# Projection stage of a hybrid encoder layer: gates in turns with two units, heads queued behind products, the gMLP gate's input kept in SBUF, five late units behind the norm

## The chip, the cores and the metric

The kernel runs on one core of a Trainium2 chip. The metric is the device time of one execution in microseconds; less is better. Three runs of the kernel before took 1433.87, 1438.87 and 1436.48 us, median 1436.48. One execution was also profiled.

The engines are named as the profile names them: PE is TensorE (matmuls), PEld its weight load, DVE VectorE, ACT ScalarE, POOL GpSimd, SP SyncE, which issues all transfers here. Every engine runs its own instructions in order, and so does SP with its queue of transfers.

## The reference

One layer of a streaming encoder for two request groups, 1024 prompt tokens and 32 sample tokens, with the same weights, all in float32:

```python
mod = silu(c) @ w_ada + b_ada
sh1, sc1, g1, sh2, sc2, g2 = split(mod, 6)
h = x * (1 + sc1) + sh1
mq, mk, mv, mo, mi, mf, fq, fk, fv, ff, gu, gv = split(h @ w_in)
hm = head_norm(mlstm(mq, mk / 8, mv, mi, log_sigmoid(mf))) * norm_g * sigmoid(mo)   # 4 heads of 64, a carried state
hf = softmax(fq fk^T / 8 + F_t - F_s, causal) fv                                    # 8 heads of 64, F = cumsum(log_sigmoid(ff))
vn = layer_norm(gv);  hg = gu * (tril(ws) @ vn + bs)                                # gMLP, in blocks of 128 tokens
x = layer_norm(ALPHA * x + (1 + g1) * (concat(hm, hf, hg) @ w_o))
h = x * (1 + sc2) + sh2
x = layer_norm(ALPHA * x + (1 + g2) * ((silu(h @ w_gate) * (h @ w_up)) @ w_down))
```

The width is 1024, the inner width of the last line 2816. Outputs are x, the new keys, values and log-forget values, the mlstm state, and vn of the sample tokens.

## The kernel before

The program is recorded with a scheduler: the code below gives a priority by the place at which an instruction is written, and the scheduler makes of it one fixed order for each engine. What stands in the code first therefore need not run first; what counts is the order on each engine.

**Products.** Every float32 operand is split into a high and a low part, so a product is three matmuls for each of the 8 slices of 128 rows (k): high by high, high by low, low by high (`gemm`, lines 114 to 116; in `tm_unit` lines 279 to 281). Weights come 512 KB at a time into one of three `raw` buffers; ACT casts the high part (line 102, `whi`) and DVE or POOL subtracts the low part (line 103, `wlo`), three buffers each.

**The stages, in the order of time.** (1) `fm_first` streams x, makes h and multiplies the first unit. (2) The projection stage: units of 128 or 256 weight columns (`fm_unit` with the features on partitions, `tm_unit` with the tokens on partitions), the gates (`gates`, lines 383 to 491, chains of small DVE operations), the pieces of the modulation (`ada`), and, with high priority between them, the attention heads for the first 512 tokens (`fox`, f0 to f7) and the mlstm blocks m0 to m3. The string `ORDER` gives their written order: q0 to q7 are the units of queries and keys of a head, k0 and k1 the mlstm keys, s the state's loads, v and o the mlstm values and output gates, a one piece of the modulation. Then follow four units of the gMLP part, two for its gate input gv (`evac_gv`) and two for gu (`evac_gmlp`), over nine tiles of tokens. (3) `wo(0)`: the output projection for the first 512 tokens, in 8 steps m, two cuts of 256 tokens. (4) The first norm (`ln1`), with "late units" as fill for PE. A late unit is the second token group's part (512 to 1056) of the queries and keys of one head; only the heads below `QD` = 2 do both groups at once. Of the six late units `PRE` - `QD` stand ahead of `wo`, the rest behind the norm. (5) The FFN (`up`, `down`) with the other attention chunks between its products, then the same for the second group.

**Around wo.** Heads, mlstm and gMLP store their results to DRAM (`dmix0` for the first 512 tokens, `dmix1` for the others), the mlstm blocks and the gMLP through two transposes and a copy (`to_mix`, lines 623 to 634, tiles `mlstm_t` and `mixs`). `wo_res` loads the residual x into z (tile `mlstm_z`, eight loads of 256 KB), `wo_mix` loads the 16 tiles of 128 x 256 through four buffers (`wo_tmp`) and splits them into `mlstm_ah` and `mlstm_al` (lines 884 and 885). `wo` uses k in the order

```python
KORDER = (2, 3, 4, 5, 0, 1, 6, 7)
```

where 2 to 5 are the attention heads, 0 and 1 mlstm, 6 and 7 gMLP. After each step, `sublayer_end` adds the result to z (line 923), before it the pivot of the norm is subtracted on POOL (line 920).

**The gate input.** `evac_gv` normalises a tile on DVE, scales and shifts it on POOL (lines 350, 351) and stores it to `dvn` in DRAM; `evac_gmlp` loads it again (tile `gvn`) for its four small matmuls (line 646).

Of the kernel before, what the change touches and what calls it, by code (L numbers as in the profile page):

```python
# [33 lines left out]
PRE = 4  # L34
# [8 lines left out]
ORDER = "q0 f0 q1 a f1 a q2 f2 k0 k1p s a q3 f3 a v q4 f4 a q5 f5 o a m0 q6 f6 a m1 q7 m2 f7 a m3"  # L43
# [24 lines left out]
class Kernel:  # L68
# [39 lines left out]
    def gemm(self, ps, w, cols, xh, xl, start=True, stop=True):  # L108

        nc = self.nc  # L110
        n = len(w)
        for k in range(n):
            hi, lo = w[k][0][:, cols], w[k][1][:, cols]
            nc.tensor.matmul(ps, hi, xh(k), start=start and k == 0, stop=False)  # L114
            nc.tensor.matmul(ps, hi, xl(k), start=False, stop=False)  # L115
            nc.tensor.matmul(ps, lo, xh(k), start=False, stop=stop and k == n - 1)  # L116
# [223 lines left out]
    def evac_gv(self, tt, ps, n):  # L340
# [7 lines left out]
        v = self.t(self.sm, [P, 256], F32, "traw", 2)  # L348
# [3 lines left out]
        self.store(self.dvn[:n, tt, :], v[:n])  # L352
# [30 lines left out]
    def gates(self):  # L383
# [19 lines left out]
        nc.vector.scalar_tensor_tensor(p, p, 1.0, s, ALU.add, ALU.mult)  # L403
        nc.vector.tensor_scalar(a, z, 0.0, None, ALU.min)
# [3 lines left out]
        self.store(d["o_lfs"], ls[:NS, 8, 4:12])  # L408
        gs = t([P, 9, 96], "gs")
# [8 lines left out]
        for j0 in (0, 4, 8):  # L418
# [6 lines left out]
            nc.scalar.copy(rb[:, j0:j0 + nj, :].rearrange("p j q -> p (j q)"), ps[:96, :nj * P])  # L425

# [4 lines left out]
        for j in range(8):  # L431
# [7 lines left out]
            self.store(self.dfs[:, :, j * P:(j + 1) * P], f(fr[64:72]))  # L439
        nc.vector.tensor_copy(self.sf[64:72, :], rb[64:72, 8, 0:NS])  # L440

# [6 lines left out]
        for i in range(7):  # L448
            w = 1 << i
            dst = tmp[i % 2]  # L450
            nc.vector.tensor_tensor(dst[:, :, w:], src[:, :, w:], src[:, :, :P - w], ALU.max)
            nc.gpsimd.tensor_copy(dst[:, :, :w], src[:, :, :w])
            src = dst
        A = src
# [16 lines left out]
        self.store(d["o_ms"], mes)  # L471
        m0x = t([4, 9], "m0x")
# [39 lines left out]
    def mlstm(self, j):  # L512
# [97 lines left out]
        sq = t([P, 4, 64], "msq")  # L610
# [304 lines left out]
    def sublayer_end(self, c, z, m, ps, gate, st, a, b):  # L915
# [3 lines left out]
        if pivot and m:  # L919
            self.nc.gpsimd.tensor_tensor(z[:, m, sl], z[:, m, sl], st["pv"][:, sl], ALU.subtract)  # L920
# [6 lines left out]
        if st and st["sum"]:  # L927
# [125 lines left out]
    def run(self):  # L1053
# [9 lines left out]
        self.dvn = t([P, 9, 256], "dvn")  # L1063
# [52 lines left out]
        self.gates()  # L1116
        more(T1[3])
        s2 = ExitStack()
# [3 lines left out]
        def emit(x):  # L1122
# [7 lines left out]
            if x[0] == "q":  # L1130
                self.fm_unit(w3[2 + i], self.evac_qk(i), (0, 1) if i < QD else (0,), eng)
            elif x[0] == "k":
                self.fm_unit(w3[i], self.evac_mqk(2 + i, 0.125), eng=eng)
# [36 lines left out]
        for h in range(QD, PRE):  # L1170
            self.fm_unit(w3[2 + h], self.evac_qk(h), (1,))
# [10 lines left out]
        for h in range(PRE, 8):  # L1182
            self.fm_unit(w3[2 + h], self.evac_qk(h), (1,))
# [179 lines left out]
```

## Time and profile before

| | us |
|---|---|
| median of 3 runs | 1436.48 |
| lowest and highest run | 1433.87, 1438.87 |
| the profiled execution | 1436.1 |
| its span, first to last instruction | 1434.3 |
| PE busy in it | 1385.6 (97%) |
| DVE busy | 960.7 (67%) |
| ACT busy | 641.3 (45%) |
| POOL busy | 254.3 (18%) |
| mean granted TensorE clock | 0.986 |

How to read the views. A group's row has the line of the code, the engine, the operation, the tiles it writes and reads, their shapes, the count, and then busy us, mean ns and the idle time ahead of it. "PE fm_g L114 <- DVE fm_qkl L364" in the waits means that PE's matmul at line 114 waited for DVE's instruction at line 364. Matmuls are pipelined: one of 256 columns takes about 0.28 us from start to end, but the next starts 0.12 us after it. The clock is the share of the full TensorE clock that was granted, 1.00 at the best.

### The profile page before, as it was taken

The page shows a single profiled execution, that of the slowest core. Times are in us where ns is not written, and L with a number is a line of the kernel's source. Part 1 is how long each engine was busy: PE and PEld are TensorE (multiplying, and loading weights), DVE is VectorE, ACT ScalarE, POOL GpSimd, SP SyncE. Part 2 cuts the span into 40 slices and gives each one's busy share as a digit, 9 for nine tenths or more (in the row PEclk, how much of TensorE's full clock was granted, in tenths as well). Part 3 has the DMA queues.
Part 4 walks back from the last instruction along what each step waited for, and adds up shares of the span by engine and source line. Part 5 has one row for each costly group of instructions (what it writes and reads, how often), then busy time and mean ns, then how long its engine had stood idle before and what let it go on. Part 6 is the DMA issues. An engine that isn't in the chain of part 4 may idle for free.

```text
span 1434.3 us, 28877 instructions
## 1 busy us (share of the span) xinstructions
PE 1385.6 (97%) x11141; PEld 1336.3 (93%) x11141; DVE 960.7 (67%) x2220; ACT 641.3 (45%) x1405; POOL 254.3 (18%) x295
## 2 busy tenths in 40 slices
PE   7999999999999899999999999999999999999994
PEld 4899988989899889999999998999999999999994
DVE  5558655678688777687767765668857545454676
ACT  3323244434445564546555353436745342424353
POOL 0103100043157300000000002254500000000433
PEclk9999999999999999999999999999999999999997
DMA  9754678565654755443443533522224222222431
GB/s 359 253 210 128 200 206 259 160 197 168 224 176 151 215 161 178 115 145 120 126 139 104 101 104 67 196 89 74 100 73 153 89 89 89 89 89 89 133 104 63
DMA packets 120867, 207.35 MB, mean 145 GB/s; under 512 B 21380, under 2 KB 76300, under 8 KB 120728
## 3 DMA queue, kind: packets, MB, share of 16 engines
q1 hardware_dynamic: 120728, 205.49, 45.9%
q8 instruction: 88, 1.44, 0.4%
q14 instruction: 51, 0.42, 0.1%
HBM read 173.78 MB, written 31.66 MB: 143 GB/s over the span
## 4 chain that ended last, share of the span: by engine, by line
PE 82%; DMA 7%; DVE 6%; ACT 1%; issue 1%; SPq 1%; POOL 1%; DVEq 0%; ACTq 0%; POOLq 0%
PE up_g L115 8%; PE up_g L116 8%; PE up_g L114 8%; PE dn_g L114 4%; PE dn_g L115 4%; PE dn_g L116 4%; PE up_u L116 3%; PE up_u L115 3%; PE up_u L114 3%; PE tm_g L279 2%; PE tm_g L280 2%; PE tm_g L281 2%; PE fox_t L729 2%; PE wo_g L114 2%; PE wo_g L115 2%; PE wo_g L116 2%
## 5 line engine op out<-in xcount | busy, mean ns | idle before, releaser
L114 PE MATMUL up_g<-wo_ah,up_whi 128*128 128x256 f32 (+1 forms) x1008 | 288.8, 287 | 3.4 <-ACT lna_tmp L942 3.3
L115 PE MATMUL up_g<-wo_al,up_whi 128*128 128x256 f32 (+1 forms) x1008 | 290.4, 288 | 0.4 <-DVE wo_al L945 0.4
L116 PE MATMUL up_g<-wo_ah,up_wlo 128*128 128x256 f32 (+1 forms) x1008 | 289.4, 287 | 0.0
L114 PEld LDWEIGHTS up_g<-wo_ah,up_whi 128*128 128x128 f32 x1008 | 191.4, 190 | 4.9 <-ACT wo_ah L944 3.5
L115 PEld LDWEIGHTS up_g<-wo_al,up_whi 128*128 128x128 f32 x1008 | 191.6, 190 | 1.3 <-DVE wo_al L945 0.7
L116 PEld LDWEIGHTS up_g<-wo_ah,up_wlo 128*128 128x128 f32 x1008 | 191.3, 190 | 0.4 <-DVE up_wlo L103 0.2
L102 ACT CAST up_whi<-up_raw 128x1024 fp32r<-128x1024 f32 x94 | 98.5, 1047 | 143.1 <-PE dn_u L115 53.8
L103 DVE TENSOR_TENSOR up_wlo<-up_raw,up_whi 128x1024 fp32r<-128x1024 f32 x94 | 121.1, 1288 | 61.0 <-ACT up_whi L102 60.7
L114 PE MATMUL dn_g<-up_acth,dn_whi 128*128 128x256 f32 (+1 forms) x464 | 133.8, 289 | 2.4 <-DVE mlstm_z L923 2.4
L115 PE MATMUL dn_g<-up_actl,dn_whi 128*128 128x256 f32 (+1 forms) x464 | 132.3, 286 | 0.0
L116 PE MATMUL dn_g<-up_acth,dn_wlo 128*128 128x256 f32 (+1 forms) x464 | 132.1, 285 | 0.0
L116 PE MATMUL up_u<-wo_ah,up_wlo 128*128 128x272 f32 (+1 forms) x400 | 115.4, 289 | 0.0
L114 PE MATMUL up_u<-wo_ah,up_whi 128*128 128x272 f32 (+1 forms) x400 | 114.9, 287 | 0.0
L115 PE MATMUL up_u<-wo_al,up_whi 128*128 128x272 f32 (+1 forms) x400 | 114.5, 286 | 0.0
L280 PE MATMUL tm_g<-tm_wlo,start_h1h 128*128 128x256 f32 (+1 forms) x384 | 111.3, 291 | 0.0
L281 PE MATMUL tm_g<-tm_whi,start_h1l 128*128 128x256 f32 (+1 forms) x384 | 111.0, 290 | 0.0
L279 PE MATMUL tm_g<-tm_whi,start_h1h 128*128 128x256 f32 (+1 forms) x384 | 110.3, 289 | 0.2 <-ACT tm_mixs L630 0.2
L114 PE MATMUL fm_g<-start_h1h,fm_whi 128*128 128x256 f32 (+2 forms) x344 | 102.7, 304 | 5.5 <-ACT fm_whi L102 1.9
L115 PE MATMUL fm_g<-start_h1l,fm_whi 128*128 128x256 f32 (+2 forms) x344 | 102.5, 298 | 0.1
L116 PE MATMUL fm_g<-start_h1h,fm_wlo 128*128 128x256 f32 (+2 forms) x344 | 101.4, 296 | 0.0
L114 PEld LDWEIGHTS dn_g<-up_acth,dn_whi 128*128 128x128 f32 x464 | 87.7, 189 | 3.3 <-DVE mlstm_z L923 3.0
L115 PEld LDWEIGHTS dn_g<-up_actl,dn_whi 128*128 128x128 f32 x464 | 87.8, 189 | 0.4
(447 smaller groups left out, 3806.2 us busy)
## 6 DMA issues: line engine op xcount, KB each, us to landing
up_raw<-w_gu SPq DMA_DIRECT2D x94, 512.0 KB
dn_raw<-w_dn SPq DMA_DIRECT2D x30, 512.0 KB
ada_late<-w_ada SPq DMA_DIRECT2D x24, 512.0 KB
wo_raw<-w_o SPq DMA_DIRECT2D x24, 512.0 KB
ada_araw<-w_ada SPq DMA_DIRECT2D x16, 512.0 KB
fm_raw<-w_in_f SPq DMA_DIRECT2D x16, 512.0 KB
tm_raw<-w_in SPq DMA_DIRECT2D x12, 512.0 KB
dn_raw<-w_dn SPq DMA_DIRECT2D x16, 384.0 KB
```

The source lines that it names most:

```text
L102: nc.scalar.copy(hi[:, :w], raw[:, :w])
L103: (eng or nc.vector).tensor_tensor(lo[:, :w], raw[:, :w], f(hi[:, :w]), ALU.subtract)
L114: nc.tensor.matmul(ps, hi, xh(k), start=start and k == 0, stop=False)
L115: nc.tensor.matmul(ps, hi, xl(k), start=False, stop=False)
L116: nc.tensor.matmul(ps, lo, xh(k), start=False, stop=stop and k == n - 1)
L279: nc.tensor.matmul(ps[:, :ncol], xh, hi, start=k == 0, stop=False)
L280: nc.tensor.matmul(ps[:, :ncol], xh, lo, start=False, stop=False)
L281: nc.tensor.matmul(ps[:, :ncol], xl, hi, start=False, stop=k == 7)
L729: nc.tensor.transpose(ps[:, y * P:(y + 1) * P], probs[y][:, b * P:(b + 1) * P], self.ident)
```

## The change

- **Gates in turns.** `gates` becomes a generator with fourteen stops, and `fm_unit` one with a stop after each range; the two units q0 and q1 are written in turns with the gates.
- **Heads queued behind products.** `ORDER` is new: q0 and q1 are out of it, heads stand at other places, and m3 is the last again, now without a piece of the modulation ahead of it. Each head is written with `issue_after(self.lastmm.ins)`: the scheduler may place its instructions only behind the last matmul of the last `gemm` written so far.
- **The gate input in SBUF.** The normalised tile stays in a pool of its own (`vk`, five buffers); the tensor `dvn` with its nine stores and nine loads is gone. To make room the mlstm's squares (`msq`) share the buffer of `mkw`, the weighted keys that the state's matmul reads.
- **Five late units behind the norm.** `PRE` is 3 where it was 4: one late unit stands ahead of `wo`, five behind the norm.
- **The pivot.** Where the norm's sums are not taken (the last group but one of `down`), the pivot is subtracted behind the addition instead of ahead of it.

```diff
-PRE = 4
+PRE = 3
...
-ORDER = "q0 f0 q1 a f1 a q2 f2 k0 k1p s a q3 f3 a v q4 f4 a q5 f5 o a m0 q6 f6 a m1 q7 m2 f7 a m3"
+ORDER = "f0 a q2 f1 a k0 k1p s f2 a q3 v f3 a q4 o f4 a q5 m0 f5 q6 a m1 q7 f6 a m2 f7 m3"
...
-            nc.tensor.matmul(ps, lo, xh(k), start=False, stop=stop and k == n - 1)
+            self.lastmm = nc.tensor.matmul(ps, lo, xh(k), start=False, stop=stop and k == n - 1)
...
             evac(o, n, ps[:, :n])
+            yield
+            self.phase = "fm"
...
-        v = self.t(self.sm, [P, 256], F32, "traw", 2)
+        v = self.vn[tt] = self.t(self.vk, [P, 256], F32, "vn", 5)
         nc.vector.tensor_scalar(v[:n], ps[:n, :256], mv[:n, 0:1], r[:n], ALU.subtract, ALU.mult)
         nc.gpsimd.tensor_tensor(v[:n], v[:n], self.rowp[:n, 272:528], ALU.mult)
         nc.gpsimd.tensor_tensor(v[:n], v[:n], self.rowp[:n, 528:784], ALU.add)
-        self.store(self.dvn[:n, tt, :], v[:n])
...
             nc.vector.tensor_tensor(x[:, tt, :], self.G[:, tt, :], self.rowp[:, 0:16], ALU.add)
+        yield
+        self.phase = "gates"
...
-        sq = t([P, 4, 64], "msq")
+        sq = t([P, 4, 64], "mkw")
...
-        vn = self.t(self.sm, [P, 256], F32, "gvn", 2)
-        self.load(vn[:n], self.dvn[:n, tt, :])
+        vn = self.vn[tt]
...
-        if pivot and m:
-            self.nc.gpsimd.tensor_tensor(z[:, m, sl], z[:, m, sl], st["pv"][:, sl], ALU.subtract)
+        sums = st and st["sum"]
+        less = lambda: self.nc.gpsimd.tensor_tensor(z[:, m, sl], z[:, m, sl], st["pv"][:, sl], ALU.subtract)
+        if pivot and m and sums:
+            less()
...
         if pivot and m == 0:
             self.ln_pivot(st, z, sl)
-        if st and st["sum"]:
+        elif pivot and not sums:
+            less()
+        if sums:
             self.ln_sum(st, z, m, sl)
...
-        self.gates()
+
+        def units(*hs):
+            for h in hs:
+                yield from self.fm_unit(w3[2 + h], self.evac_qk(h))
+
+        weave(self.gates(), units(0, 1))
         more(T1[3])
+        s7 = ExitStack()
+        self.vk = self.pool("vk", ctx=s7, side="right")
+        self.vn = {}
...
-            if x[0] in "fm" and HPA:
-                with tc.high_priority(HPA):
-                    weave(*[iter(emit(y)) for y in x.split("+")])
-            else:
-                weave(*[iter(emit(y)) for y in x.split("+")])
+            with ExitStack() as how:
+                if x[0] in "fm":
+                    how.enter_context(tc.high_priority(HPA))
+                if x[0] == "f":
+                    how.enter_context(tc.issue_after(self.lastmm.ins))
+                weave(iter(emit(x)))
```

What the scheduler makes of it, at two places. The first is PE around the last mlstm block, m3, and the start of the output projection. `mlstm_t` from `mlstm_mhm` are the two transposes with which m3 hands over its result; `wo_g` are the output projection's products, `fm_g` those of a late unit, `tm_g` those of the gMLP units. Before, at PE's rows 2353 to 2359, while the first wo_g stands at row 2500:

```order
L580 MATMUL mlstm_s_4280<-mlstm_mv_817_4243,mlstm_mkw_4267 128x130 x2
L628 MATMUL mlstm_t_4311<-start_ident_101,mlstm_mhm_4291 128x128 x2
L182 MATMUL ada_t_4216<-start_ident_101,ada_adas_4229 128x128 x2
L628 MATMUL tm_g_4971<-start_ident_101,tm_traw_4998 128x128 x2
L628 MATMUL tm_g_5013<-start_ident_101,tm_traw_5040 128x128 x2
L279 MATMUL tm_g_5097<-tm_whi_4961,start_h1h_151 128x256
L280 MATMUL tm_g_5097<-tm_wlo_4962,start_h1h_151 128x256
```

And in the change, at rows 2448 to 2459 (line 649 is the old line 628):

```order
L649 MATMUL mlstm_t_4292<-start_ident_100,mlstm_mhm_4272 128x128 x2
L115 MATMUL fm_g_5192<-start_h1l_151,fm_whi_5154 128x272
L116 MATMUL fm_g_5192<-start_h1h_150,fm_wlo_5155 128x272
L114 MATMUL fm_g_5192<-start_h1h_150,fm_whi_5154 128x272
L115 MATMUL fm_g_5192<-start_h1l_151,fm_whi_5154 128x272
L116 MATMUL fm_g_5192<-start_h1h_150,fm_wlo_5155 128x272
L114 MATMUL fm_g_5192<-start_h1h_150,fm_whi_5154 128x272
L115 MATMUL fm_g_5192<-start_h1l_151,fm_whi_5154 128x272
L116 MATMUL fm_g_5192<-start_h1h_150,fm_wlo_5155 128x272
L182 MATMUL ada_g_5131<-start_ident_100,ada_adas_5144 128x128 x2
L114 MATMUL wo_g_5265<-mlstm_ah_832_4318,wo_whi_5261 128x256
L114 MATMUL wo_g_5302<-mlstm_ah_832_4318,wo_whi_5298 128x256
```

m3's transposes, which had 136 product matmuls between them and the first wo_g, have 8; and the products of the steps m = 0, 1 and 2 now alternate over k (5265, 5302 and a third are their banks).

The second place is SP's queue at the same point. `start_dmix` from `mlstm_mixs` is the store of m3's result (12_68 and 11_67 are dmix0, 13_69 is dmix1), `mlstm_z` from `xT` the residual, `wo_tmp` the tiles for the output projection. Before:

```order
L88 DMA start_dmix_12_68<-fox_fr_4212 64x512
L85 DMA tm_gvn_5122<-start_dvn_63 128x256
L88 DMA start_dmix_12_68<-mlstm_mixs_4314 128x2x128
L88 DMA start_dmix_13_69<-tm_mixs_5010 128x2x128
L88 DMA start_dmix_13_69<-tm_mixs_5052 128x2x128
L85 DMA mlstm_z_837_4328<-xT 128x512 x8
L85 DMA wo_tmp_4341<-start_dmix_12_68 128x256
L85 DMA wo_tmp_4345<-start_dmix_12_68 128x256
L85 DMA wo_tmp_4349<-start_dmix_12_68 128x256
L85 DMA wo_tmp_4353<-start_dmix_12_68 128x256
L85 DMA tm_gvn_5160<-start_dvn_63 32x256
```

And in the change:

```order
L88 DMA o_kT<-fm_qkr_5185 64x272
L88 DMA start_dmix_11_67<-mlstm_mixs_4295 128x2x128
L85 DMA mlstm_z_831_4309<-xT 128x512 x8
L85 DMA wo_tmp_4322<-start_dmix_11_67 128x256
L85 DMA wo_tmp_4326<-start_dmix_11_67 128x256
L85 DMA wo_tmp_4330<-start_dmix_11_67 128x256
L85 DMA wo_tmp_4334<-start_dmix_11_67 128x256
L88 DMA start_dqh_57<-fm_qkh_5217 128x272
L88 DMA start_dql_58<-fm_qkl_5218 128x272
L88 DMA o_kT<-fm_qkr_5219 64x272
L85 DMA wo_raw_5444<-w_o 128x1024
```

In both, the residual and the tiles follow m3's store; the loads of `tm_gvn` are gone, a late unit's three stores and one weight load of the output projection stand behind the first four tiles, and the other twelve tiles follow in one piece.

More of the change, by code (lines that the diff above doesn't have):

```diff
@@ L403, in gates @@
         nc.vector.scalar_tensor_tensor(p, p, 1.0, s, ALU.add, ALU.mult)
+        yield
+        self.phase = "gates"
         nc.vector.tensor_scalar(a, z, 0.0, None, ALU.min)
@@ L408, in gates @@
         self.store(d["o_lfs"], ls[:NS, 8, 4:12])
+        yield
+        self.phase = "gates"
         gs = t([P, 9, 96], "gs")
@@ L425, in gates @@
             nc.scalar.copy(rb[:, j0:j0 + nj, :].rearrange("p j q -> p (j q)"), ps[:96, :nj * P])
+        yield
+        self.phase = "gates"
         fc = t([72, 8], "fc")
@@ L439, in gates @@
             self.store(self.dfs[:, :, j * P:(j + 1) * P], f(fr[64:72]))
+            if j % 2:
+                yield
+                self.phase = "gates"
         nc.vector.tensor_copy(self.sf[64:72, :], rb[64:72, 8, 0:NS])
+        yield
+        self.phase = "gates"
         m0s = t([4, 1], "m0s")
@@ L453, in gates @@
             src = dst
+            if i % 2:
+                yield
+                self.phase = "gates"
+        yield
+        self.phase = "gates"
         A = src
@@ L471, in gates @@
         self.store(d["o_ms"], mes)
+        yield
+        self.phase = "gates"
         m0x = t([4, 9], "m0x")
@@ L1170, in run @@
         for h in range(QD, PRE):
-            self.fm_unit(w3[2 + h], self.evac_qk(h), (1,))
+            weave(self.fm_unit(w3[2 + h], self.evac_qk(h), (1,)))
+        s7.close()
         s6.close()
@@ L1182, in run @@
         for h in range(PRE, 8):
-            self.fm_unit(w3[2 + h], self.evac_qk(h), (1,))
+            weave(self.fm_unit(w3[2 + h], self.evac_qk(h), (1,)))
         self.ln1_res(0)
```

5 lines of the change are left out of this document (2 added, 3 removed).

## The prediction

> **What bounds the kernel now.** I read the page first, then the waits of TensorE (PE), then the clock around each wait, and last the transfers ahead of the output projection.
>
> ```profile
> span 1434.3 us, 28877 instructions
> PE 1385.6 (97%) x11141; PEld 1336.3 (93%) x11141; DVE 960.7 (67%) x2220; ACT 641.3 (45%) x1405; POOL 254.3 (18%) x295
> PE 82%; DMA 7%; DVE 6%; ACT 1%; issue 1%; SPq 1%; POOL 1%; DVEq 0%; ACTq 0%; POOLq 0%
> ```
>
> PE is busy for 97% of the span and the chain that ended last runs over it. The change leaves the number of products as it is, so it can win only what PE loses in gaps, and lose only by new gaps. These are the waits of PE from 40 to 560 us, in us in total, times, longest, and below the "..." those from 860 to 900 us:
>
> ```profile
> PE up_g L114 <- ACT lna_tmp L942: 3.3, 1, 3.3
> PE fox_t L729 <- DVE fox_p L715: 2.3, 1, 2.3
> PE fm_g L114 <- DVE fm_qkl L364: 1.9, 1, 1.9
> PE fox_s L698 <- DMA fox_qp<-start_dql: 1.8, 2, 1.6
> PE tm_g L646 <- DMA tm_gvn<-start_dvn: 1.5, 1, 1.5
> PE fm_g L114 <- ACT tm_mixs L630: 0.9, 1, 0.9
> PE fox_s L698 <- DMA fox_qp<-start_dqh: 0.6, 1, 0.6
> ...
> PE dn_g L114 <- DVE mlstm_z L923: 2.4, 2, 1.8
> ```
>
> A gap costs more than itself. In the view by stretches (start:end, length, busy time and count on PE, PEld, DVE, ACT and POOL, granted clock, DMA share, GB/s) the first two rows are the gap at 139 us and what follows it; 305:309 and 473:477 hold the gaps at 306 and 474 us, and the rest follow the gaps at 242, 306, 378, 474 and 887 us:
>
> ```profile
> 138.00:142.00 4.00, 2.11 (x18) 1.91 (x17) 3.91 (x7) 0.14 (x1) 1.55 (x2) 1.00 0.30 91
> 142.00:146.00 4.00, 4.00 (x23) 4.00 (x22) 3.88 (x5) 1.87 (x4) 3.55 (x7) 0.57 0.32 93
> 245.00:249.00 4.00, 4.00 (x24) 4.00 (x24) 2.52 (x11) 1.39 (x5) 0.00 (x0) 0.62 0.94 300
> 305.00:309.00 4.00, 1.74 (x12) 1.31 (x11) 3.96 (x10) 1.28 (x4) 2.59 (x2) 1.00 0.74 226
> 309.00:313.00 4.00, 4.00 (x24) 4.00 (x22) 3.27 (x8) 0.97 (x2) 2.02 (x4) 0.57 0.77 276
> 381.00:385.00 4.00, 4.00 (x21) 4.00 (x21) 1.45 (x5) 1.13 (x3) 0.00 (x0) 0.57 0.81 263
> 473.00:477.00 4.00, 1.04 (x9) 0.83 (x8) 4.00 (x9) 2.80 (x8) 2.44 (x2) 0.96 0.10 37
> 477.00:484.00 7.00, 6.27 (x36) 5.60 (x40) 5.29 (x14) 5.47 (x15) 7.00 (x12) 0.53 0.50 144
> 890.00:894.00 4.00, 3.35 (x29) 3.15 (x28) 0.97 (x2) 0.00 (x0) 4.00 (x6) 1.00 0.66 37
> ```
>
> PE looks fully busy in 142:146, but it does 23 matmuls there at a clock of 0.57: (1 - 0.57) x 4 = 1.7 us are lost on top of the 1.9. After 242 us it is 0.38 x 4 = 1.5, after 306 and 378 us 1.7 each, after 474 us 0.47 x 7 = 3.3; after 887 us nothing (1.00). What the change can win at most is therefore 242: 1.6 + 1.5, 306: 2.3 + 1.7, 378: 1.5 + 1.7 with 0.9 just before it, 474: 3.3 + 3.3, 887: 2.4, and 0.6 at the first head: 20.8 us.
>
> **The gates in turns.** The order of all five engines is the same before and after up to PE's row 1102 (about 175 us), so the weaving of the gates with q0 and q1 moves nothing, and the gap at 139 us stays with its 1.9 + 1.7. I cost this part at 0; no other work has to hide it.
>
> **The gate input in SBUF.** Nine stores and nine loads of up to 128 KB go from SP's queue. The gap of 1.5 us is PE waiting for such a load. What the stores did to SP between 330 and 410 us:
>
> ```profile
> SPq L88 <- POOL tm_traw L351: 12.9, 5, 3.6
> ```
>
> SP, an engine in order, stood 12.9 us behind POOL's affine step, with loads queued behind the stores. Now PE waits for POOL alone, whose result is ready before any of these stores could start. I take the whole 0.9 + 1.5 + 1.7 = -4.1 (bounds -4.1 and 0). The squares of mlstm now share a buffer with mkw and wait for the state's matmul; between that one and the transposes of m3 PE has 40 late-unit products in the new order, about 5 us, that hide this. Without that cover it would be part of the new waits below.
>
> **Heads behind products.** The heads' matmuls stand later behind the products of the unit ahead. Gaps of 0.6 + 3.1 + 4.0 = 7.7 us at the heads can go; I take -5 (bounds -7.7 and 0), since a head that starts later is also packed closer to the next one. The stage's end is denser: f7 and m3 run with few products between their steps. New waits there cost what the old ones did, 3.1 to 4.0 us each with the clock. I take +2.5, less than one; bounds 0 and 8 (two).
>
> **The wait ahead of the output projection.** This is the largest term. m3 is now last, and SP issues the residual (mlstm_z) and every wo_tmp load only after m3's store. The old times of that chain, in the timeline (start, length, engine, operation; SP, ACT and PE rows, left-out rows between them):
>
> ```profile
> 365.70 0.38 PE L628 MATMUL mlstm_t<-start_ident,mlstm_mhm 128*128 128x128 f32 x2
> ...
> 366.52 0.37 SPq L88 DMA_DIRECT2D start_dmix<-mlstm_mixs  x1
> 366.98 0.96 SPq L88 DMA_DIRECT2D start_dmix<-tm_mixs  x2
> 368.03 3.76 SPq L85 DMA_DIRECT2D mlstm_z<-xT  x8
> 371.84 2.55 SPq L85 DMA_DIRECT2D wo_tmp<-start_dmix  x4
> ...
> 377.35 1.51 ACT L884 CAST mlstm_ah<-wo_tmp 128x256 fp32r<-128x256 f32 x4 [2.31 <-DMA wo_tmp<-start_dmix]
> ...
> 378.24 1.75 SPq L85 DMA_DIRECT2D wo_tmp<-start_dmix  x4
> ...
> 382.90 1.13 ACT L884 CAST mlstm_ah<-wo_tmp 128x256 fp32r<-128x256 f32 x3 [3.39 <-DMA wo_tmp<-start_dmix]
> 383.79 1.27 SPq L85 DMA_DIRECT2D wo_tmp<-start_dmix  x3
> ...
> 386.41 0.40 ACT L884 CAST mlstm_ah<-wo_tmp 128x256 fp32r<-128x256 f32 x1
> ```
>
> And wo's own matmuls in the first nine microseconds, in the view by stretches (PE, PEld, DVE, clock, DMA share, GB/s):
>
> ```profile
> 391.40:400.40 9.00, 8.67 (x72) 8.51 (x72) 0.48 (x1) 1.00 0.60 189
> ```
>
> Before, the transposes of m3 (365.70) lay 26 us ahead of wo's first matmul (391.4 to 391.5), and product work covered the chain. Now 8 products stand between. Let T be the start of m3's transposes. The store is issued at T + 0.8 (366.52 - 365.70) and takes 0.4, so the residual's first load goes at T + 1.3; the two stores of tm_mixs that stood between are gone. From there to the first cast took 377.35 - 368.03 = 9.3: T + 10.6, and with a cast and a subtraction of 0.4 each the first tile is usable at T + 11.4. There are four tmp buffers, so 16 tiles come in rounds of four. A round is 386.41 - 383.79 = 2.6 plus 0.8, or 3.4; with two 512 KB weights ahead, 382.90 - 378.24 = 4.7 plus 0.8, or 5.5. wo's products take k in the order 2, 3, 4, 5, 0, 1, 6, 7, and k = 6 and 7 are tiles 13 and 14, three rounds after the first: one weight stands in the queue, so half the extra, 11.4 + 3 x 3.4 + 1 = T + 22.6.
>
> PE is done with the 8 products at about T + 1.4 and has m = 0, 1, 2 to do: 72 products in 8.7 us by the last row, 54 of them (6.5 us) for the first six k. Unhindered it would ask for k = 6 at T + 7.9. The loss is 22.6 - 7.9 = 14.7, in two gaps of some 9 and 5 us, and the half clock of 1.7 after the second; the one after the first lies within the wait for the second. So +16.4. Low bound: tmp lands 2.6 after its issue as z's last load goes (371.84 - 368.03 + 2.6, plus 1.3: T + 7.7, usable 8.5) and rounds stay 3.4, giving 10.8. High: two rounds of 5.5 and 3.3 for the clock, giving 18 + 3.3 = 21. Queued behind on SP are only wo's later weights, which cannot be converted before m = 0 has freed its buffers.
>
> **The fifth late unit.** It leaves the stretch ahead of wo and comes back behind the norm, 5.8 us each way, so the move itself is 0. It fills the 474 us gap:
>
> ```profile
> 457.00:463.00 6.00, 6.00 (x50) 6.00 (x49) 0.50 (x1) 1.14 (x3) 1.00 0.36 113
> L364 DVE SCALAR_TENSOR_TENSOR fm_qkl<-fm_g,start_qsc,fm_qkh 128x272 fp32r<-128x272 f32 x8 | 3.9, 493 | 3.4 <-POOL mlstm_z L954 2.2 <-POOL fm_qkr L365 1.1
> L103 DVE TENSOR_TENSOR fm_wlo<-fm_raw,fm_whi 128x1024 fp32r<-128x1024 f32 x3 | 3.6, 1215 | 0.1
> ```
>
> Fifty such matmuls took 6.0 us, so a unit's 48 (two ranges, eight k, three each) take 5.8, more than the gap. But DVE is the one that is late there (4.00 of 4.00 in 473:477), and the unit gives it 1.2 + 2 x 0.5 = 2.2 us more. Of 6.6 us I take -4.6 (bounds -6.6 and -2.6).
>
> **The subtraction behind the addition.** In the down stage DVE's addition (L923) no longer waits for POOL's subtraction of the pivot where no sums follow. The 2.4 us at 887 go: -2.4 (bounds -2.4 and 0). POOL's subtraction is late next, and nobody asks for it before the last group.
>
> **The sum.** -4.1 - 5 + 2.5 + 16.4 - 4.6 - 2.4 = +2.8 on the profiled execution's 1436.1 (span 1434.3), which lies 0.4 under the runs' median of 1436.48. The forecast is 1439, a change of 0.2%: within the 0.3% (4.3 us) below which a measurement of this kernel cannot tell it from none.
>
> **The clock by the skill.** The Trainium skill, "TensorE: Matmul & The Clock Gate", Part 1, puts the halved clock behind an idle window of about 3.4 us and states the rule that PE be kept free of gaps longer than that. The trace disagrees: gaps of 1.5 to 2.3 us are followed by 0.57 to 0.62 for some 4 us. By the rule the gaps that go would be worth only themselves, and the sum would be the fourth rival's.
>
> **Rivals.** (1) *Slower: the stage's end starves.* One mechanism: f7, m2 and m3 packed in the last products ahead of wo; DVE's small steps queue, m3 comes late, and each us of that adds in full to the wait for wo because nothing covers it any more. For it speaks that DVE was at 3.96 of 4.00 where head and units met at 306 us (the row is the wait of fox_t on fox_p); against it, that DVE had idle time beside another head (2.52 of 4.00 in 245:249). It decides once m3 is over 5 us late. New waits at 8 and the wait for wo at its high 21: +2.8 + 5.5 + 4.6 = 1449. (2) *Faster: the wait is short.* The loads meet an empty queue, wo's wait costs 10.8 and all the gaps go: 10.8 - 4.1 - 7.7 + 0 - 6.6 - 2.4 = -10: 1426; with part of it, 1428. For: 300 GB/s moved at 245 us, 189 around wo; against: DVE's load behind the norm. (3) *The parts do not do what they say*: so it is for the gates, which is in every case. Were the heads' part as empty, their -5 would be gone: 1444, inside the forecast's own range. (4) *Gaps without aftermath.* If the half clock would be there without the gaps, because it comes at its own times, the wins lose 1.7 at 378, 5/7.7 of 3.2 at the heads and 4.6/6.6 of 3.3 behind the norm, 6.1 in all: 1445. Against: each of five such stretches follows a gap.
>
> **How the numbers follow.** Forecast 0.37 (its own range 1432 to 1444: same 0.22, slower 0.12, faster 0.03); rival 1 0.27, slower; rival 2 0.26, faster; rival 4 0.10, slower. Together faster 0.29, same 0.22, slower 0.49. The middle of the largest case stays the prediction. The range takes in most of rivals 1 and 2: 1427 to 1452, with a tenth left out on either side.
>
> **What would show it.** Right: PE waits in wo's first products for a wo_tmp cast, one of about 9 and one of about 5 us, some 20 us after the transposes of m3, with a clock near half behind them; the gap at 139 us unchanged; no wait on tm_gvn or on L923 near 887 us; the wait on lna_tmp under 2 us. Wrong: m3's store long ahead of wo's first matmul; or waits of PE in the heads over 8 us in sum; or a half clock without a gap before it.

## The result, and the profile after

Four runs of the changed kernel took 1444.84 to 1454.52 us, median 1450.47; four of the kernel before, median 1435.17. The ratio is 1.0098, 95% interval 1.0073 to 1.0122: the change makes the kernel slower by 1%. The time lies in the range of the prediction, at the time of its first rival, not of its forecast.

| | before | after |
|---|---|---|
| median, us | 1435.17 | 1450.47 |
| profiled execution, us | 1436.1 | 1448.55 |
| its span, us | 1434.3 | 1446.4 |
| its mean granted clock | 0.986 | 0.983 |

The head of the page, after:

```profile
span 1446.4 us, 28825 instructions
PE 1384.2 (96%) x11141; PEld 1336.1 (92%) x11141; DVE 961.5 (66%) x2220; ACT 642.4 (44%) x1405; POOL 258.2 (18%) x295
```

PE did the same 11141 matmuls and was busy for 1.4 us less, so all of the 12.1 us by which the span grew is waiting. The waits of PE from 40 to 600 us (total, times, longest):

```profile
PE wo_g L114 <- ACT mlstm_ah L904: 9.4, 2, 7.8
PE up_g L114 <- DVE fm_qkl L365: 3.5, 1, 3.5
PE fox_s L718 <- DMA fox_k<-start_dqh: 3.0, 1, 3.0
PE fox_o L754 <- DVE fox_ptl L753: 2.0, 1, 2.0
PE fox_s L719 <- DMA fox_k<-start_dql: 2.0, 1, 2.0
PE fm_g L114 <- DVE fm_qkl L365: 2.0, 1, 2.0
PE ada_g L182 <- ACT ada_adas L179: 1.7, 1, 1.7
PE fox_s L719 <- DMA fox_k<-start_dqh: 1.4, 1, 1.4
```

The first row is new and the largest: the output projection waits for its tiles. The second stands where the old wait on lna_tmp stood and is as long; the third, the first mixer head's wait for its keys, is new. The waits on tm_gvn and, near 887 us, on the addition into z are gone. The sixth is the gap at 139 us, unchanged. Here is the chain ahead of the output projection, from the timeline (PE, ACT and SP rows; line 649 is the old 628, line 904 the old 884):

```profile
381.12 0.38 PE L649 MATMUL mlstm_t<-start_ident,mlstm_mhm 128*128 128x128 f32 x2
...
381.93 0.38 SPq L88 DMA_DIRECT2D start_dmix<-mlstm_mixs  x1
382.36 3.98 SPq L85 DMA_DIRECT2D mlstm_z<-xT  x8
...
386.38 2.15 SPq L85 DMA_DIRECT2D wo_tmp<-start_dmix  x4
...
391.94 1.45 ACT L904 CAST mlstm_ah<-wo_tmp 128x256 fp32r<-128x256 f32 x4 [7.83 <-DMA wo_tmp<-start_dmix]
...
402.81 1.88 ACT L904 CAST mlstm_ah<-wo_tmp 128x256 fp32r<-128x256 f32 x4 [1.12 <-DMA wo_tmp<-start_dmix]
...
403.27 0.62 PE L114 MATMUL wo_g<-mlstm_ah,wo_whi 128*128 128x256 f32 x3 [1.60 <-ACT mlstm_ah L904]
```

With T = 381.12 the residual's loads start at T + 1.2 (forecast 1.3), the first cast at T + 10.8 (10.6), and PE gets k = 6 at T + 22.2 (22.6). The stretches there and behind the norm, with the clock in the third column from the end:

```profile
384.00:393.00 9.00, 1.04 (x5) 0.81 (x6) 3.32 (x13) 1.17 (x5) 0.97 (x2) 0.54 0.98 331
393.00:397.00 4.00, 4.00 (x20) 4.00 (x20) 0.87 (x3) 0.56 (x3) 0.00 (x0) 0.50 0.77 252
404.00:408.00 4.00, 3.13 (x22) 2.58 (x22) 3.23 (x6) 3.45 (x5) 0.00 (x0) 1.00 0.00 0
142.00:146.00 4.00, 4.00 (x23) 4.00 (x23) 3.88 (x5) 2.00 (x4) 3.48 (x6) 0.57 0.32 93
```

While PE stood, the DMA engines were at 0.98 of their time and moved 331 GB/s: the wait is transfers. The first products then ran at half clock (0.50), which cost nothing of its own, because the next tiles were not there before 403 us.

Where the 12.1 us came from, at equal work. Wo's last matmul starts at 441.4 us before and 446.5 after, the first matmul of down at 540.7 and 553.0; k = 6 before is reckoned as 391.5 + 6.5. A late unit's 48 matmuls, 5.8 us, moved from ahead of the output projection to behind it, so 5.8 is added to times ahead of it and taken from the stretch behind:

| stretch of the profiled execution | before | after | difference at equal work |
|---|---|---|---|
| start to the end of the products ahead of wo | 391.5 | 382.5 | 382.5 + 5.8 - 391.5 = -3.2 |
| from there to wo's k = 6 | 6.5 | 20.8 | +14.3 |
| from k = 6 to wo's last matmul | 43.4 | 43.2 | -0.2 |
| to the first matmul of down | 99.3 | 106.5 | 7.2 - 5.8 = +1.4 |
| to the end | 893.6 | 893.4 | -0.2 |

These are two executions, one of each kernel. The point-by-point part below sets them beside executions of other runs, and there the first row does not hold.

### The profile page after: what moved, and what is told of

Read it like the earlier page. It is cut to its first block, busy times and chain, and to the rows that moved or that the text cites. A ratio compares the mean times of both kernels' runs of the same rounds, so it can differ in the third digit from the quotient of the medians.

```text
span 1446.4 us, 28825 instructions
## 1 busy us (share of the span) xinstructions
PE 1384.2 (96%) x11141; PEld 1336.1 (92%) x11141; DVE 961.5 (66%) x2220; ACT 642.4 (44%) x1405; POOL 258.2 (18%) x295
## 4 chain that ended last, share of the span: by engine, by line
PE 84%; DMA 6%; DVE 5%; ACT 2%; SPq 1%; issue 1%; POOL 1%; DVEq 0%; ACTq 0%; POOLq 0%
PE up_g L116 8%; PE up_g L115 8%; PE up_g L114 8%; PE dn_g L114 4%; PE dn_g L115 4%; PE dn_g L116 4%; PE up_u L116 3%; PE up_u L115 3%; PE up_u L114 3%; PE tm_g L281 3%; PE tm_g L282 3%; PE tm_g L283 3%; PE fm_g L114 3%; PE fm_g L115 2%; PE fm_g L116 2%; PE fox_t L749 2%
```

## The experiments

Twelve kernels were run, in three groups of four beside runs of the kernel before (medians 1437.1 to 1437.6 us there). The change itself was not run again beside them. Differences to it are between medians of different groups; by the ratios they come out the same within 0.5 us. The waits and stage times of a run are those of its one profiled execution, which lay up to 6.3 us from the run's median (u_pre: 1435.49 us, x_res2: 1439.18, both the fastest of their run).

| run | median us | ratio to before, 95% interval |
|---|---|---|
| x_res | 1449.69 | 1.0091 (1.0073 to 1.0109) |
| u_order | 1441.34 | 1.0037 (1.0019 to 1.0056) |
| u_pre | 1441.78 | 1.0037 (1.0016 to 1.0058) |
| vn_pivot | 1436.63 | 1.0002 (0.9989 to 1.0015) |
| x_res2 | 1444.59 | 1.0057 (1.0032 to 1.0083) |
| vn_pivot_res2 | 1436.81 | 1.0003 (0.9988 to 1.0018) |
| o_pre | 1439.99 | 1.0017 (1.0000 to 1.0033) |
| o_pivot | 1434.34 | 0.9973 (0.9958 to 0.9988) |
| u_pre_res2 | 1446.51 | 1.0067 (1.0048 to 1.0086) |
| o_order | 1445.01 | 1.0058 (1.0037 to 1.0080) |
| o_vn | 1444.96 | 1.0054 (1.0036 to 1.0071) |
| pivot_norm | 1435.76 | 0.9986 (0.9965 to 1.0007) |

**x_res: the residual's loads behind the first tile loads, in the changed kernel.**

```diff
-        self.wo_res(0, self.pz)
         self.operand(0, self.ph)
         self.wo_mix(0, self.KORDER[:6])
+        self.wo_res(0, self.pz)
```

> The changed kernel with one thing other: the sixteen tile loads for the output projection (wo_tmp) are written ahead of the eight residual loads (mlstm_z), so that SP issues the tiles right behind m3's store. Theory 1, the wait ahead of the output projection is the transfer chain behind m3's store: without the 2.1 MB ahead of them the first tiles land about 6 us earlier (3.8 us of issue and the moving), so the first wait of 7.8 us falls to about 2 us and the kernel takes about 1444 us. Theory 2, m3 itself is late and the transfers matter little: the wait stays over 6 us and the time at 1449 to 1452. Theory 3, most of the loss sits in the heads and behind the norm: the wait falls, but the time by less than 3 us.

1449.7 us, no gain. The waits of PE in this run:

```profile
PE wo_g L114 <- ACT mlstm_ah L904: 7.4, 2, 6.7
```

There are still two waits, but the long one is now the second. m3's transposes came 3.3 us later in this execution (T = 384.4 us); the output projection starts at T + 4.2 instead of T + 11.3 and its last matmul at T + 64.0 instead of T + 65.4. SP's rows show why: the scheduler put two of the eight residual loads behind the first four tiles, three behind eight and three behind twelve, so that the whole 2.1 MB still stood ahead of the last four tiles. By its numbers theory 2 held (7.4 us of wait, 1449.7 us), but the edit took the residual only out of the first tiles' way and put it in the later ones': it moved the wait and tells nothing of its cause. x_res2 below moves it further back.

**u_order: the old ORDER in the changed kernel.**

```diff
-ORDER = "f0 a q2 f1 a k0 k1p s f2 a q3 v f3 a q4 o f4 a q5 m0 f5 q6 a m1 q7 f6 a m2 f7 m3"
+ORDER = "f0 a f1 a q2 f2 k0 k1p s a q3 f3 a v q4 f4 a q5 f5 o a m0 q6 f6 a m1 q7 m2 f7 a m3"
```

> The changed kernel with the old ORDER (heads and mlstm blocks at their old places, q0 and q1 with the gates as in the change). m3's transposes then have 48 product matmuls behind them ahead of the output projection instead of 8, 40 x 0.12 = 4.8 us more cover. Theory 1 (the wait is what costs): the wait of 7.8 us falls to about 3 us, and the new waits in the heads (1.4, 2.0, 0.8 and 2.0 us, with their half clock) go back to the old ones: 1440 to 1445. Rival (the order is not the cause; the five late units and the norm are): 1448 to 1452.

1441.3 us, 9 us less than the change, in the range of theory 1. The wait for the tiles is 8.4 us in sum, not 3, but it falls earlier: wo's last matmul is at 437.6 instead of 446.5 us, because the heads' waits are smaller (PE's waits from 40 to 375 us are 6.1 us in sum; in the change 10.9, in x_res and x_res2 with the same order 8.7 and 10.5) and the products ahead of wo are done at 375.5 us instead of 382.5 (x_res 385.8, x_res2 380.9). From there to wo's last matmul it takes 62.1 us, in the change 64.0: the gain lies ahead of wo, not at the tiles. So the time came as expected and half of the reason given for it did not.

**u_pre: PRE = 4 in the changed kernel.**

```diff
-PRE = 3
+PRE = 4
```

> The changed kernel with PRE = 4: two late units ahead of the output projection, four behind the norm, as before. 48 matmuls (5.8 us) more stand between m3's transposes and the output projection. Theory 1: the first wait falls from 7.8 to about 2 us, and the unit's 5.8 us are taken back behind the norm, where the old gap of 3.3 us with its half clock returns: -6 for the wait, 0 to +3 behind the norm, 1444 to 1447. Rival (the fifth unit behind the norm costs by itself, by the wait of up_g on fm_qkl of 3.5 us and the first mixer head's wait of 3.0 us for its keys): 1440 to 1443.

1441.8 us, 8.7 less than the change: less time than theory 1 had, in the range of its rival. What both name is in the trace. wo's last matmul comes at 443.0 us against 446.5 + 5.8 = 452.3 at equal work, so the unit ahead covers transfers; and the wait of up_g on fm_qkl is gone and that of the first mixer head down to 0.7 us, while the old one on lna_tmp (3.4 us) is back. The profiled execution is 6.3 us faster than the run's median, so these stages tell where the gain lies and not how large it is.

**vn_pivot: the kernel before with the gate input in SBUF and the pivot behind the addition.**

```diff
+        v = self.vn[tt] = self.t(self.vk, [P, 256], F32, "vn", 5)
-        self.store(self.dvn[:n, tt, :], v[:n])
-        sq = t([P, 4, 64], "msq")
+        sq = t([P, 4, 64], "mkw")
+        vn = self.vn[tt]
...
+        elif pivot and not sums:
+            less()
```

> The kernel before with two parts of the change alone: the gate input in SBUF (with the shared buffer of the squares) and the subtraction of the pivot behind the addition. If the parts are worth what the prediction took them for, -4.1 and -2.4: about 1429 us, the gaps at 374, 378 and 887 us gone, and m3's transposes still 96 matmuls (11.5 us) ahead of the output projection, which nearly covers its loads. Rival: the gate input's tiles move other work, a new wait of the same size comes in its place and only the pivot's 2.4 us stay: about 1433 us. Third: m3 later than before opens a wait ahead of the output projection of some 5 us: about 1435 to 1438 us.

1436.6 us, as before. The waits on tm_gvn and at 887 us are gone, and PE waits 5.0 us for the first tile of the output projection: m3's transposes stand 96 instead of 136 matmuls ahead of it. That is the third expectation, in wait and time.

**x_res2: the residual's loads written behind all tile loads, in the changed kernel.**

```diff
-        self.wo_res(0, self.pz)
         self.operand(0, self.ph)
...
         self.wo_mix(0, self.KORDER[6:])
+        self.wo_res(0, self.pz)
```

> The changed kernel with the residual's loads (mlstm_z) written behind all sixteen tile loads of the output projection; the run before had them behind the first four or so only, and the wait had moved from the first products (7.8 to 0.7 us) to the later tiles (6.7 us). Theory 1 (the wait ahead of the output projection is the transfers behind m3's store, rounds of four tiles included): the first wait stays under 1 us and the wait for the later tiles falls from 6.7 to about 3 us (three rounds of 3.4 us against 6.5 us of products): together 3 to 4 us instead of 9.4, the kernel 5 to 7 us faster than the change, 1443 to 1446 us. Rival (the time ahead of the output projection is set by m3's own lateness, the transfers only fill it): both waits together stay over 7 us, and the time at 1449.

1444.6 us, 5.9 under the change, as theory 1 had it. The waits of PE:

```profile
PE wo_g L114 <- ACT mlstm_ah L904: 4.7, 2, 4.0
PE fox_s L718 <- DMA fox_k<-start_dqh: 4.7, 1, 4.7
```

From 9.4 to 4.7 us at the tiles, with the same order on PE up to there; from the end of the products ahead to wo's last matmul it took 56.6 us instead of 64.0. In the order made, two residual loads stand ahead of the last four tiles and six behind all. So the transfers behind m3's store set the wait, not m3's lateness. The first mixer head's wait of 4.7 us stays.

**vn_pivot_res2: the same move in vn_pivot.** The edits are those of vn_pivot and x_res2.

> The kernel before with the gate input in SBUF and the pivot behind the addition, and in addition the residual's loads behind the tile loads. In the run with the two parts alone the gap at 887 us and the waits on tm_gvn were gone, but PE waited 5.0 us for the first tile and the time was that of the kernel before. If that wait is what ate the two gains: it falls under 1 us, and the time is 1430 to 1432 us, faster than before. Rival (the new order of the heads costs what the gates' input wins): the wait goes, but the time stays at 1434 to 1437 us, or another wait opens for the residual at the first sublayer end.

1436.8 us, as without it. The wait for tiles fell from 5.0 to 1.1 us, and these came up:

```profile
PE wo_g L114 <- ACT wo_whi L102: 3.3, 1, 3.3
PE wo_g L114 <- DVE fm_qkl L363: 1.2, 1, 1.2
```

The rival held in its time, and another wait did open, though not for the residual, as it had it: now the projection's weights, loaded behind tiles and residual, are late. Residual, tiles and weights share one queue and one window of time, and here the choice of which stands last only changed the name of the wait.

**o_pre: PRE = 3 alone, in the kernel before.**

```diff
-PRE = 4
+PRE = 3
```

> The kernel before with PRE = 3 alone: one late unit moved from ahead of the output projection to behind the norm. The prediction took this for -4.6 us (a unit fills the gap of 3.3 us at 474 us and its half clock). The changed kernel shows another mechanism: the unit's evacuation stands in DVE's queue behind eight multiplications of the norm, so that PE waits 3.5 us for a bank, and the first mixer head waits 3.0 us for its keys. If that comes with the unit itself: a wait of up_g on fm_qkl of 3 us and one of fox_s on fox_k of 2 to 3 us here too, and 88 instead of 136 matmuls between m3 and the output projection open a small wait there (11 us of 22 covered): 1438 to 1443 us. If the prediction's step was right: 1430 to 1433 us.

1440.0 us, ratio 1.0017 (1.0000 to 1.0033): at most a small loss, where the prediction had a gain of 4.6. The waits of PE, beside 1.7 us for a tile of the output projection:

```profile
PE fox_s L698 <- DMA fox_k<-start_dqh: 3.9, 1, 3.9
PE up_g L114 <- DVE fm_qkl L364: 2.9, 1, 2.9
```

Both waits of the changed kernel come with the fifth unit itself. Why up_g waits for fm_qkl is seen in the changed kernel's DVE rows of the timeline:

```profile
475.62 3.97 DVE L962 TENSOR_TENSOR mlstm_z<-mlstm_z,wo_pv 128x256 f32<-128x256 f32 x8
479.51 1.42 DVE L963 TENSOR_TENSOR mlstm_z<-mlstm_z,wo_qs 128x256 f32<-128x256 f32 x4
480.85 1.21 DVE L103 TENSOR_TENSOR up_wlo<-up_raw,up_whi 128x1024 fp32r<-128x1024 f32 x1
481.98 0.49 DVE L365 SCALAR_TENSOR_TENSOR fm_qkl<-fm_g,start_qsc,fm_qkh 128x272 fp32r<-128x272 f32 x1
```

PE was through with the late units at 479.0 us. The evacuation that frees a bank for up_g stands in DVE's queue behind 6.6 us of the norm's and the next weights' work, and the first up_g starts at 482.5. Its other half stands behind the norm as well, in ACT's queue: the high part, from which DVE's subtraction is made, follows three of the norm's steps, which had waited for DVE.

```profile
479.96 1.58 ACT L966 ACTIVATE lna_tmp<-mlstm_z,wo_lnb,wo_lng 128x256 f32<-128x256 f32 x3 [5.62 <-DVE mlstm_z L963]
481.44 0.47 ACT L364 ACTIVATE fm_qkh<-fm_g,start_qsc 128x272 fp32r<-128x272 f32 x1
```

**o_pivot: the subtraction behind the addition alone, in the kernel before** (the second half of vn_pivot's diff).

> The kernel before with the pivot's subtraction behind the addition alone. If the gap at 887 us is worth its 2.4 us: 1433 to 1434 us, with no wait on L923 there. Rival (the time moves into another wait in the same stage, as the run of the whole change hints, whose stretch from the first down group to the end took as long as before): 1435 to 1437 us, with a wait of 1 us or more that was not there between 820 and 930 us.

1434.3 us, ratio 0.9973 (0.9958 to 0.9988), the one part that makes the kernel faster; 2.7 us between the medians, where 2.4 were expected. No wait on the addition near 887 us is left, and none of 1 us came up between 820 and 930 us, where the rival had one.

**u_pre_res2: the changed kernel with PRE = 4 and the residual behind the tiles.**

> The changed kernel with two things undone or moved: PRE = 4 again, and the residual's loads behind the tile loads. PRE alone gave 1441.8 us with 6.0 us of waits for tiles left, the loads alone 1444.6 us. If these two places hold the loss of the change (the fifth unit behind the norm, the transfers behind m3's store) and they add: 48 more matmuls cover the rest of the transfers, the waits for tiles are under 1 us, the waits of up_g on fm_qkl and of the first mixer head for its keys are gone: 1434 to 1438 us, the time of the kernel before. Rival (a third place, the new waits in the heads, holds some 4 us or more): 1440 to 1443 us.

1446.5 us, over both expectations and 4.7 over u_pre. The output projection waits for weights now, beside 3.6 us for a tile (u_pre: 6.0 for tiles):

```profile
PE wo_g L114 <- ACT wo_whi L102: 2.3, 1, 2.3
PE wo_g L116 <- DVE wo_wlo L103: 1.3, 2, 0.7
```

The two remedies don't add. Where the late unit covers the tiles, putting the residual between them and the weights makes the weights late. In the profiled executions this is only a part of the loss: from the end of the products ahead to wo's last matmul it took 59.1 us against 57.5 in u_pre, and from the first matmul of down to the end 895.9 against 891.3. What holds the rest of the 4.7 us stays open.

**o_order: the new ORDER alone, in the kernel before** (q0 and q1 written ahead, then the change's string).

> The kernel before with the new ORDER alone (q0 and q1 written ahead, then the change's string). It says what the new places of heads and mlstm blocks are worth with everything else as before. 106 matmuls (12.7 us) stand between m3's transposes and the output projection. The prediction took -5 us for the heads and +2.5 for new waits: 1433 to 1435 us, if the cover holds. Rival (the new places only trade old waits in the heads for new ones): 1436 to 1439 us. Third (m3's lateness opens a wait for the tiles of 3 us or more): 1440 us or more.

1445.0 us, ratio 1.0058: the third expectation's time, but by other waits than the one it named. PE doesn't wait for tiles; it waits for the weights of the output projection, and in the heads:

```profile
PE wo_g L114 <- ACT wo_whi L102: 4.9, 3, 1.8
PE wo_g L116 <- DVE wo_wlo L103: 3.0, 4, 0.8
PE fox_s L698 <- DMA fox_qp<-start_dqh: 2.0, 1, 2.0
PE fox_s L698 <- DMA ada_late<-w_ada: 1.5, 1, 1.5
```

**o_vn: the gate input in SBUF alone, in the kernel before** (the first half of vn_pivot's diff).

> The kernel before with the gate input in SBUF alone. With the pivot's subtraction it gave 1436.6 us, and the pivot alone 1434.3. If they add, this part alone is worth nothing or costs 2 us: 1437 to 1440 us, with the waits on tm_gvn gone and 3 to 5 us of wait for the first tile of the output projection in their place. Rival (the two do not add, the part itself saves the 4.1 us of the prediction): 1432 to 1434 us.

1445.0 us, over all expectations: alone this part costs 7 us, with the pivot's edit the two together nothing. The wait of 4.9 us for the first tile is there as in vn_pivot. What vn_pivot doesn't have is one wait of PE of 5.6 us far behind, in the sample block of mlstm (the timeline, PE, DVE, ACT, PE):

```profile
885.85 0.83 PE L579 MATMUL mlstm_s<-mlstm_mv,mlstm_mkw 32*128 32x130 f32 x4
886.72 1.19 DVE L586 SCALAR_TENSOR_TENSOR fm_Cs<-fm_Cs,fm_d0c,mlstm_s 64x65 f32<-64x65 f32 x4 [1.87 <-PE mlstm_s L579]
...
889.08 0.41 ACT L610 ACTIVATE mlstm_mkw<-mlstm_mhm 32x256 f32<-32x256 f32 x1 [2.87 <-DVE mlstm_mhm L608]
...
892.25 0.42 PE L627 MATMUL mlstm_t<-start_ident,mlstm_mhm 32*128 32x32 f32 x2 [5.57 <-DVE mlstm_mhm L617]
```

The squares (L610) now write the buffer that the state's matmul (L579) reads, and in the order made here the rest of DVE's normalisation of the block, from the mean at 887.9 us on, stands behind the state's update (L586, 886.7 us), which waits for that matmul. By then PE has nothing but the transposes to go on with. In the kernel before the squares were taken at 879.7 us and the transposes done at 885.9. Whether PE has to wait depends on where the scheduler has put the transposes: in vn_pivot and in the changed kernel it doesn't. That the shared buffer makes this order is read off the trace; no run gives the squares their own buffer back and keeps the rest.

**pivot_norm: an attempt at more, o_pivot with every second addition of the first norm on POOL.**

```diff
-            (nc.gpsimd if k % 4 == 1 else nc.vector).tensor_tensor(zk, zk, e, ALU.add)
+            (nc.gpsimd if k % (4 if c else 2) == 1 else nc.vector).tensor_tensor(zk, zk, e, ALU.add)
```

> An attempt at a version that beats both: the kernel before with the pivot behind the addition, and in the first norm the addition of every second k on POOL instead of every fourth. DVE was busy for 4.00 of 4.00 us at the gap of 474 us; two of its additions of 0.4 us a cut go to POOL. If DVE's own work sets that gap: the wait on lna_tmp falls from 3.4 to about 2 us, 1432 to 1434 us. Rival (POOL's addition of 0.8 us and the wait for it are in the chain then): no change from the pivot alone, 1434 to 1437 us.

1435.8 us, 0.9986 (0.9965 to 1.0007): nothing gained on o_pivot. The wait on lna_tmp is gone and a wait of up_g on fm_qkl of 4.0 us stands in its place.

Not run: the gates in turns and the heads' queueing. Up to the first heads the order of the change is that of before, as the prediction said; and without the line that queues the heads behind the last product the scheduler gives the same order on all engines, row for row, so that part too moves nothing.

## Why the prediction was right and wrong, point by point

**The wait ahead of the output projection: right, in mechanism and size.** Forecast 14.7 us of loss in two gaps and 1.7 of half clock; measured 14.3 and no half clock behind the second gap (1.00 in 404:408). The gaps were 1.7 (for a piece of the modulation), 7.8 and 1.6. The last is shorter than the 5 forecast because the products before it ran at half clock (0.50) and so filled time in which PE would have waited. x_res2 shows that the transfers behind m3's store make it.

**The gates: right.** The gap at 139 us and the 0.57 behind it are there, to the hundredth.

**The fifth late unit: wrong, in the step "it fills the 474 us gap".** Forecast -4.6, measured +1.4 behind wo, and o_pre alone gives a loss of 2.9 us between the medians. PE's matmuls were long enough to fill the gap; the step that failed is that the unit was charged 2 us of the 6.6, for DVE's 2.2 us more, as if that were all it asked of the late engine. Its evacuation stands in one queue with the norm, on DVE and on ACT, so that the bank for the next products is freed behind the norm's work, and the first mixer head waits for the keys that the unit stores. This is clear of the spread between executions: from wo's last matmul to the first of down it took 105.5 to 108.3 us in the five runs with the fifth unit (the change, x_res, x_res2, u_order, o_pre), 99.7 to 102.5 without its 5.8, and 99.2 to 101.0 in the eight with four units (pivot_norm, which alters the norm, left out). A gain of 4.6 is in none of them.

**Heads and gate input: wrong, in the step that took the gaps of one execution as the kernel's price.** Forecast -4.1 - 5 + 2.5 = -6.6; the table above has PE 3.2 us earlier at the end of the products ahead of wo. But up to some 12 us ahead of the first wo_g all five engines have the same order in o_pivot and pivot_norm as in the kernel before, and in x_res and x_res2 as in the change. The products ahead of wo ended at 391.5, 388.7 and 385.8 us in the first three, and at 382.5, 385.8 and 380.9 in the others, or 388.3, 391.6 and 386.7 at equal work. The means are 0.2 us apart: of the 6.6 us nothing is seen, and the 3.2 is chance.

The gains were counted in the profiled execution of the kernel before. The wait of 1.5 us on tm_gvn, there with 1.7 of half clock behind it, is 0.3 us in pivot_norm and not there in o_pivot, though both load the gate input from DRAM; and in pivot_norm no half clock follows the head's wait at 306 us:

```profile
PE tm_g L646 <- DMA tm_gvn<-start_dvn: 0.3, 1, 0.3
308.00:312.00 4.00, 4.00 (x37) 4.00 (x36) 3.87 (x10) 0.97 (x2) 2.02 (x4) 1.00 0.91 298
```

In the change the old waits of the heads are smaller and new ones stand in their place (2.0, 2.0 and 1.4, where +2.5 had been set): between 170 and 381 us the sum of all waits rose from 7.3 to 8.8 us. In u_order, with the old ORDER, these three are not there. o_order and o_vn show that neither part wins alone. The shared buffer, costed at nothing under the cover of 40 products at m3, was costed at one place only. It counts for every mlstm block: 5.6 us at the last one in o_vn. And a wait of a mixer's fox_s on the exponential near 833 us (1.2 us in the change, 1.3 to 2.1 in eight others) is in every run with the gate input in SBUF and in none without it; what in the part makes it wasn't tried.

**The pivot: right where it was placed** (o_pivot 2.7 us, 887 us clear), but the change didn't keep it: its stretch from down to the end is 0.2 us shorter, not 2.4, with that wait near 833 us in it. Eight executions have the gate input and the pivot: there this stretch took 891.3 to 896.8 us, in the mean 893.8, against 893.6 to 894.7 in the three with neither and 889.7 and 891.3 in the two with the pivot alone.

**The sum:** 2.8 forecast, 12.1 measured in the profiled execution: -2.1 at wo's wait and -0.2 behind it, +3.4 ahead of it, +6.0 behind the norm, +2.2 to the end. With the six executions above, the +3.4 is +6.8, and the sum 15.5, near the 15.3 between the medians. The time is the first rival's, but its mechanism is not: m3 wasn't late. Its result was ready at 378.3 us, 2.8 us before PE's order came to the transposes. So the excess over the forecast lay in the gains that did not come, ahead of wo, behind the norm and at the end. That the range holds the time is owed to its width, and as far as the mechanism goes it is luck. One sign came true by name alone: the wait on lna_tmp is under 2 us, since a wait of 3.5 us on fm_qkl stands in its place.

Of the parts that move anything, alone in the kernel before, three cost (ORDER 7.5 us between the medians, gate input 7.4, late unit 2.9) and one wins (pivot 2.7). Their sum, 15.1, is near the measured 15.3, but not for the same reasons: o_vn's largest wait isn't in the change, o_order waits for weights where the change waits for tiles, and undoing either ORDER or PRE in the change takes back some 9 us each, the one mostly in the heads, the other mostly at the tiles. What beats both kernels is the pivot alone.

## What to carry to other kernels

A gap that one execution shows is not yet a price: profile the same program more than once, and count as a gain only the waits that come back. A gap of PE is filled by work that doesn't pass through the engine that is late: look at which queue the filler's evacuation stands in before counting its matmuls. Before taking work away from ahead of a stage, count what it covers: here 26 us ahead of the output projection hid 22 us of transfers, and three edits used up the same cover: alone they left 96 (gate input), 88 (late unit) and 106 (ORDER) of the 136 products between m3's transposes and the output projection, together 8. A buffer shared to make room is a wait at every instance of the loop, so each instance has to be looked at, the last one above all.

## What was not expected of the hardware

A short gap isn't always followed by a halved clock. The prediction's rows show 0.53 to 0.62 behind five gaps of one execution. In u_pre PE was idle for 2 us in 304:308, and the clock stayed at 1.00 (first two rows). In x_res, which has the same order on all engines up to there, the same wait of 2.0 us was followed by 0.50 (last two):

```profile
304.00:308.00 4.00, 1.97 (x15) 1.38 (x13) 3.97 (x10) 1.06 (x6) 3.16 (x3) 1.00 0.63 202
308.00:312.00 4.00, 4.00 (x38) 2.96 (x37) 2.80 (x10) 0.80 (x2) 1.45 (x2) 1.00 0.79 255
...
304.00:308.00 4.00, 1.98 (x14) 1.78 (x14) 3.97 (x10) 1.34 (x6) 3.59 (x3) 0.88 0.60 194
308.00:312.00 4.00, 4.00 (x22) 1.41 (x20) 2.56 (x9) 0.58 (x1) 1.45 (x2) 0.50 0.56 191
```

Of five executions with this wait the clock fell behind it in three (the change, x_res, x_res2) and not in two (u_pre, u_pre_res2). So the 1.7 us behind a short gap are a chance, not a price. The fourth rival is right in that the wins lose them, though not in its condition, a half clock that comes without the gaps. This may be a part of the spread between executions: the change's four went from 1444.84 us at a mean clock of 0.988 to 1454.52 at 0.982. It isn't all of it, for x_res took 1450.58 us at 0.981 and 1450.99 at 0.987. The Trainium skill, "TensorE: Matmul & The Clock Gate", Part 1, says that the activity window which decides on the clock runs free of the kernel; that agrees with a gap of 2 us being punished in one execution and not in another, though no run here shows the window itself.
